# Residual rows and the low halves of the prompt's gates made by accumulating transfers from GpSimd's queue, in a fused two-batch encoder layer

## The chip, the cores and the metric

One NeuronCore of one Trainium2 chip runs the whole program. The metric is the device time of one execution in microseconds (us); lower is better. Times of runs are medians; the profile is of one execution.

Names used throughout: PE is TensorE (matrix multiply), DVE is VectorE, ACT is ScalarE, POOL is GpSimd, SP is SyncE, which issues nearly all the transfers of the kernel. PSUM holds the results of the matmuls, SBUF the operands. A "landing" is the moment when a transfer's data are there and its waiter may go on.

## The reference

Two requests, a prompt of 512 rows and a sample of 1024 rows, go through one encoder layer with shared weights, in float32. After the mixing half of the layer, each request has `x` (rows by 1024). The part that matters here is the gated MLP and what follows it:

```python
h = _rmsnorm(x, norm_ffn_g[l])
u = _dwconv(h @ w_up[l], ffn_dw_w[l], ffn_dw_b[l])              # 1024 -> 5632, conv of 3 taps
x = x + (jax.nn.silu(u[..., :D_FF]) * u[..., D_FF:]) @ w_down[l]  # D_FF = 2816, back to 1024
return _rmsnorm(x, norm_final_g)
```

"Rows of x" are the `x` on the right of the third line: they are added to the down-projection's sums, and the final norm is taken of the result. "The prompt's gates" are `silu(...) * u` of the prompt, the left operand of the down-projection.

## The kernel before, in words

**Exact products from two halves.** PE multiplies a shorter float format (`F32R`). Every float32 operand is therefore split: `hi` is the operand cast to `F32R`, `lo` is operand minus `hi`. A product takes three matmuls: hi by hi, hi by lo, lo by hi. The casts are done by ACT, the subtractions by DVE or POOL.

**The down-projection** is the last phase. It works by a scheme of seven products in place of eight block products: `ORDER = (1, 2, 5, 6, 7, 4, 3)` names them, and product `i` runs over `NPAIR = 11` slices `p` of the contracted dimension. So there are 77 steps `(i, p)`. A step of the first six products has six pieces `tt` of 128 rows: four of the sample and two (`tt` 4 and 5) of the prompt, each of three 128x128 by 128x512 matmuls, 18 matmuls in all (`mm_down`). Product 3 is cut up differently at the end: pieces 0 and 1, with 4 and 5 beside them, slice by slice; then piece 2 over all slices, then piece 3.

**Operands.** `operands(i, p)` makes what a step needs. It splits a block of the sample's gates and a block (or difference of blocks) of `w_down`, both with `split_of`, whose subtraction is DVE's here. At every second `p` it also splits the prompt's gates for two slices at once, 128x512 (128x256 for the last slice): `raw` was loaded by SP from the DRAM tensors `gap...`, ACT casts it to `hi`, POOL writes `lo`. That makes 6 per product, 42 low halves in all, of which 7 are 128x256. The step that is computed is `LEAD` = 4 steps (6 in the later products; `LZ` = 6 slices in product 3) behind the one whose operands are made.

**Slots.** SBUF tiles come from a fixed set of buffers (`Slots`): 61 of 2048 bytes a partition are called `h0` to `h60`, 15 of 4096 bytes `q0` to `q14`, a few others `c` and `d`. A tile takes the longest-free slot of the smallest size that fits, and gives it back when the Python object goes, so a tile's slot is handed on in the order of the program text. In the built program `h7_1997` is the 1997th tile, in slot `h7`. The instruction that writes a slot's next tile waits until the last one's readers are done.

**Rows of x.** The mixing half stored `x` in the DRAM tensors `x1d0` to `x1d11`. Four sums, `o11`, `o12`, `e` and `u`, each three SBUF tiles of 128x1024, collect the products (`evacuate`, after each product's last slice). `load_x1` loads the rows for one sum into three tiles of their own with six transfers of 128x512 from SP; some steps later `with_x` adds them, the first tile by DVE, the others by POOL. The end (`finish`) squares, scales and stores the sums.

**Order.** PE's and SP's instructions stand in the order of the program text in this phase. The orders of ACT, DVE and POOL are set by a scheduler from its own estimates when the program is built. Each engine and each queue carries out its instructions in order: one that waits holds all behind it.

Of the kernel before, what the change touches and what calls it, by code (L numbers as in the profile page):

```python
# [9 lines left out]
F32 = mybir.dt.float32  # L10
F32R = mybir.dt.float32r
BF16 = mybir.dt.bfloat16
AF = mybir.ActivationFunctionType
ALU = mybir.AluOpType
# [4 lines left out]
NT = 512  # L19
# [89 lines left out]
def tile_hybrid_encoder(ctx: ExitStack, tc: tile.TileContext, xs, rel_bias, norm_attn_g, w_in,  # L109
                        attn_sink, conv_dw_w, conv_dw_b, conv_ln_g, conv_ln_b, w_out, norm_ffn_g,  # L110
                        w_up, ffn_dw_w, ffn_dw_b, w_down, norm_final_g, onehot, laid, outs):
    nc = tc.nc
# [8 lines left out]
    sb = Slots(lambda tag: sml if tag[0] == "s" else big,  # L121
               dict(q=(15, 4096), c=(4, 4352), h=(61, 2048), d=(2, 2304), s=(33, 64)))
# [661 lines left out]
    x1d = [dr.tile([P, D], F32, name=f"x1d{i}") for i in range(12)]  # L784
# [56 lines left out]
    def double_keys():  # L841
        for kv in range(NKV):
            for L in range(2):
                nc.gpsimd.tensor_copy(kt[1, kv][L][HD:P, :], kt[1, kv][L][0:HD, :].bitcast(F32))
                yield
# [69 lines left out]
    n, doubling = 0, double_keys()  # L915
# [59 lines left out]
    NPAIR, HT = NJ // 2, NT // 2  # L975
# [94 lines left out]
    def add(out, a, b, eng=None):  # L1070
        (eng or nc.vector).tensor_tensor(out, a, b, op=ALU.add)

    def sub(out, a, b, eng=None):
        (eng or nc.vector).tensor_tensor(out, a, b, op=ALU.subtract)  # L1074

    def split_of(src, dve=False, joint=False):
        if joint and any(f[0][0] == "q" for f in sb.free):
            both = sb.tile([2, NT], F32R, among="q")
            hi, lo = Part(both, 0), Part(both, 1)
        else:  # L1080
            hi, lo = sb.tile([NT], F32R), sb.tile([NT], F32R)
        nc.scalar.copy(hi[:], src)  # L1082
        sub(lo[:], src, hi[:].bitcast(F32), None if dve else nc.gpsimd)
        return hi, lo
# [412 lines left out]
    def load_next(n):  # L1497
        for _ in range(n):
            if ahead:
                key, p = ahead.popleft()  # L1500
                roomy = sum(f[0][0] in "qc" for f in sb.free) > 5
                if (key, p) in second_half:
                    t = second_half.pop((key, p))
                elif key in BRIEF and p % 2 == 0 and p + 1 < NPAIR and roomy:
                    both = sb.tile([2, NT])
                    t, second_half[key, p + 1] = Part(both, 0), Part(both, 1)
                    both = None
                else:
                    t = sb.tile([NT])
                pr[key, p] = t  # L1510
                what, i, n2 = key
                if what == "p":
                    both = next(k for k in gap if i in k)
                    n = min(2, NPAIR - p)
                    nc.sync.dma_start(t[:, 0:n * HT].rearrange("p (n t) -> p n t", t=HT),
                                      gap[both][:, p:p + n, both.index(i), :])
                    continue
                if what == "a":
                    src = ga[i, p][:]
                else:  # L1520
                    src = w_down[0, (2 * p + i) * P:(2 * p + i + 1) * P, n2 * NT:(n2 + 1) * NT]
                nc.sync.dma_start(t[:], src)
# [13 lines left out]
    hl, hp = {}, {}  # L1536

    def operands(i, p):

        while ("a", i, 0) not in [k for k, q in pr if q == p] or (i in need and (need[i], p) not in pr):  # L1540
            load_next(1)
        a = pr.pop((("a", i, 0), p))
        if i == 1:
            b = pr[B11, p]
        elif i == 2:
            b = pr.pop((B21, p))
        elif i == 5:
            b = pr[B12, p]
            sub(b[:], b[:], pr[B11, p][:])
        elif i == 6:  # L1550
            b = pr[B12, p]
            sub(b[:], pr.pop((B22, p))[:], b[:])
        elif i == 7:
            b = pr.pop((B11, p))
            sub(b[:], pr[B12, p][:], b[:])
        elif i == 4:
            b = pr.pop((B21, p))
            sub(b[:], b[:], pr.pop((B12, p))[:])
        else:
            b = pr.pop((B22, p))  # L1560
        joint = i == ORDER[-1]
        hl[i, p] = (split_of(a[:], True, joint), split_of(b[:], True, joint))
        if p % 2 == 0:
            n = min(2, NPAIR - p) * HT
            raw = pr.pop((("p", i, 0), p))
            hi, lo = sb.tile([NT], F32R), sb.tile([NT], F32R)
            nc.scalar.copy(hi[:, :n], raw[:, :n])  # L1567
            sub(lo[:, :n], raw[:, :n], hi[:, :n].bitcast(F32), nc.gpsimd)
            hp[i, p] = hp[i, p + 1] = hi, lo

    steps = [(i, p) for i in ORDER for p in range(NPAIR)]
    LEAD = 4
# [15 lines left out]
    pair2 = lambda: [sb.tile([W2]) for _ in range(3)]  # L1588
    xd = {}

    def load_x1(t, n):
        xd[t, n] = pair2()
        for w in range(3):
            for q in range(2):
                blk = 2 * t + q if w == 2 else 4 + 4 * t + 2 * w + q
                nc.sync.dma_start(xd[t, n][w][:, q * NT:(q + 1) * NT], x1d[blk][:, n * NT:(n + 1) * NT])

    outs_ = {}
    acc = {}
# [21 lines left out]
                add(acc["u"][w][:], z[:], acc["u"][w][:])  # L1621

    def with_x(name, t, n):
        x = xd.pop((t, n))
        for w in range(3):
            add(acc[name][w][:], acc[name][w][:], x[w][:], nc.gpsimd if w else None)

    fins = []

# [41 lines left out]
    def make(k):  # L1671
        nonlocal made
        while made <= min(k, len(steps) - 1):
            i, p = steps[made]
            operands(i, p)
            made += 1
# [5 lines left out]
    def down_step(k):  # L1682
        i, p = steps[k]
        if k > 1:
            next(rest, None)
        load_next(8 if k == 0 else 3 if len(pr) < CAP else 0)
        make(k + (LEAD + max(0, min(2, (k - 60) // 2)) if k else 1))
        late = H2 if i in LATE2 else 0
# [20 lines left out]
        if i == 6 and p == 3:  # L1709
            load_x1(0, 0)  # L1710
        if i == 6 and p == 7:
            with_x("o11", 0, 0)
        if i == 7 and p == XQ[0]:
            load_x1(0, 1)
        if i == 7 and p == XQ[1]:
            with_x("o12", 0, 1)
        if i == 4 and p == XP[0]:
            load_x1(1, 1)
            fins.append(sb.tile([D]))
            nc.sync.dma_start(fins[0][:], norm_final_g.partition_broadcast(P))  # L1720
            nc.scalar.activation(fins[0][:], fins[0][:], AF.Identity, scale=D ** 0.5)
        if i == 4 and p == XP[1]:
            with_x("e", 1, 1)
# [9 lines left out]
    for j in range(2, NJ):  # L1733
# [5 lines left out]
        if j >= NJ - 2:  # L1739
            load_next(4)  # L1740
# [45 lines left out]
    for p in range(NPAIR):  # L1786
# [16 lines left out]
        if p in OTHER:  # L1803
            blk = OTHER[p]
# [83 lines left out]
```

## Time and profile before

| what | value |
|---|---|
| median of 2 runs | 1484.05 us (1483.54 to 1484.55) |
| the profiled execution | 1487.45 us, of which the span of instructions is 1485.0 us |
| mean granted PE clock | 0.997 |
| PE busy | 1467.4 us, 99% of the span |
| DVE, ACT, POOL busy | 1115.4, 807.6, 793.0 us |
| HBM read and written | 166.83 MB and 61.10 MB |

The span runs from the first instruction to the last. Matmuls overlap, so a busy PE is one that always has a matmul under way; how fast they follow each other is their count in a stretch of time. The down-projection takes the stretch from about 1150 us to the end. In rows that group instructions, the columns are line, engine, operation, tiles written and read (slot numbers left out), shapes, count, then busy time and mean duration, then the engine's idle time just before them and what ended it.

### The profile page before, as it was taken

Reading aid. Unit: us, or ns where it says so; the run is one execution under the profiler, and the core shown is the slowest. Engines: PE = TensorE matmul, PEld = TensorE weight load, DVE = VectorE, ACT = ScalarE, POOL = GpSimd, SP = SyncE. Lnnn points to the kernel's source line nnn. Section 1 sums busy time; section 2 is a strip of 40 time slices with the busy share of each in tenths; the row PEclk is TensorE's granted clock in tenths of the full one; section 3 lists DMA queues with packets and bytes.
Section 4 is the critical chain, followed back from the end, with each engine's and each line's share of the span. In section 5 each row is a group of like instructions: output and inputs, shape, how many; then the busy total and the mean of one; then the engine's idle time right before and its main releaser. Section 6 shows DMA issues by size and latency. Waiting matters only on the chain. (4 is left out here: it accounts for less than half of the span.)

```text
span 1485.0 us, 19793 instructions
## 1 busy us (share of the span) xinstructions
PE 1467.4 (99%) x6688; PEld 1207.9 (81%) x6688; DVE 1115.4 (75%) x1500; ACT 807.6 (54%) x1432; POOL 793.0 (53%) x697
## 2 busy tenths in 40 slices
PE   9999999999999999999999999999999999999998
PEld 7788887878888888778887888888888888888886
DVE  6877845649988888675599888888886846578873
ACT  7524555467778776654564545444455553433365
POOL 3564453338779766322546666666655341135556
PEclk9999999999999999999999999999999999999999
DMA  9554331844444454663214433333332395456644
GB/s 369 196 150 144 105 105 31 257 148 142 127 137 136 132 180 142 199 206 127 72 58 142 147 130 129 122 128 122 127 127 94 146 323 168 124 189 220 225 161 162
DMA packets 124625, 228.17 MB, mean 154 GB/s; under 512 B 20420, under 2 KB 45764, under 8 KB 124397
## 3 DMA queue, kind: packets, MB, share of 16 engines
q1 hardware_dynamic: 124092, 226.37, 46.4%
q8 instruction: 52, 0.85, 0.2%
q10 hardware_dynamic: 432, 0.56, 0.1%
q14 instruction: 49, 0.39, 0.1%
HBM read 166.83 MB, written 61.10 MB: 153 GB/s over the span
## 5 line engine op out<-in xcount | busy, mean ns | idle before, releaser
L163 POOL TENSOR_TENSOR q<-q,q 128x1024 fp32r<-128x1024 f32 x66 | 158.7, 2404 | 67.1 <-ACT q L162 43.4
L1074 POOL TENSOR_TENSOR q<-q,q 128x512 fp32r<-128x512 f32 x82 | 125.8, 1542 | 123.0 <-ACT q L1207 112.6
L1074 DVE TENSOR_TENSOR h<-h,h 128x512 fp32r<-128x512 f32 (+1 forms) x161 | 137.7, 887 | 53.3 <-ACT h L1082 21.9
L1586 PE MATMUL w<-h,h 128*128 128x512 f32 x432 | 168.1, 389 | 0.0
L1584 PE MATMUL w<-h,h 128*128 128x512 f32 x432 | 168.1, 389 | 0.0
L1585 PE MATMUL w<-h,h 128*128 128x512 f32 x412 | 160.3, 389 | 0.0
L1074 POOL TENSOR_TENSOR h<-h,h 128x512 fp32r<-128x512 f32 (+1 forms) x46 | 66.7, 1452 | 142.5 <-ACT h L1567 117.8
L1221 PE MATMUL w<-h,q 128*128 128x512 f32 x350 | 138.0, 394 | 1.5 <-ACT w L1292 0.8
L1223 PE MATMUL w<-h,q 128*128 128x512 f32 x350 | 136.4, 390 | 0.2 <-POOL q L1074 0.2
L1222 PE MATMUL w<-h,q 128*128 128x512 f32 x350 | 136.4, 390 | 0.0
L1082 ACT CAST h<-h 128x512 fp32r<-128x512 f32 x116 | 69.1, 619 | 102.2 <-DVE h L1074 27.8
L315 PE MATMUL b<-h,q 128*128 128x512 f32 x312 | 123.0, 395 | 1.3 <-ACT h L461 0.7
L317 PE MATMUL b<-h,q 128*128 128x512 f32 x312 | 122.6, 393 | 0.0
L316 PE MATMUL b<-h,q 128*128 128x512 f32 x312 | 122.3, 392 | 0.0
L315 PE MATMUL u<-h,q 128*128 128x512 f32 x272 | 106.8, 393 | 0.0
L316 PE MATMUL u<-h,q 128*128 128x512 f32 x272 | 106.8, 393 | 0.0
L317 PE MATMUL u<-h,q 128*128 128x512 f32 x272 | 106.7, 392 | 0.0
L352 DVE SCALAR_TENSOR_TENSOR c<-d,cvw,c 128x512 f32<-128x512 f32 x128 | 96.0, 750 | 1.6
L162 ACT CAST q<-q 128x1024 fp32r<-128x1024 f32 x66 | 69.0, 1047 | 51.3 <-PE u L316 15.7
L344 POOL TENSOR_TENSOR h<-h,h 128x512 f32<-128x512 f32 x62 | 82.0, 1324 | 27.8 <-ACT h L343 23.4
L1584 PEld LDWEIGHTS w<-h,h 128*128 128x128 f32 x432 | 81.1, 188 | 16.8
L1586 PEld LDWEIGHTS w<-h,h 128*128 128x128 f32 x432 | 81.1, 188 | 16.7
(464 smaller groups left out, 3990.9 us busy)
## 6 DMA issues: line engine op xcount, KB each, us to landing
q<-in_laid_w_up SPq DMA_DIRECT2D x88, 512.0 KB, 3.7
ga<-q SPq DMA_DIRECT2D x65, 256.0 KB, 2.2
h<-gap SPq DMA_DIRECT2D x57, 256.0 KB, 3.8
h<-ga SPq DMA_DIRECT2D x57, 256.0 KB, 3.5
h<-in_w_down SPq DMA_DIRECT2D x52, 256.0 KB, 3.6
q<-in_laid_w_in SPq DMA_DIRECT2D x22, 512.0 KB, 4.2
gap<-h SPq DMA_DIRECT2D x44, 256.0 KB, 2.4
q<-in_x_sample SPq DMA_DIRECT2D x15, 512.0 KB, 7.0
```

What stands on the lines that cost most here:

```text
L163: (nc.vector if dve else nc.gpsimd).tensor_tensor(lo[:], raw[:], hi[:].bitcast(F32), op=ALU.subtract)
L315: nc.tensor.matmul(out, whi[:, kc, :], hi[:], start=(kc == 0), stop=False)
L316: nc.tensor.matmul(out, whi[:, kc, :], lo[:], start=False, stop=False)
L317: nc.tensor.matmul(out, wlo[:, kc, :], hi[:], start=False, stop=(kc == KC - 1))
L352: nc.vector.scalar_tensor_tensor(acc[:], src(t), w(t), acc[:], op0=ALU.mult, op1=ALU.add)
L1074: (eng or nc.vector).tensor_tensor(out, a, b, op=ALU.subtract)
L1221: nc.tensor.matmul(out, whi[:, s], hi[:], start=(start and c == 0), stop=False, **go)
L1222: nc.tensor.matmul(out, whi[:, s], lo[:], start=False, stop=False, **go)
L1223: nc.tensor.matmul(out, wlo[:, s], hi[:], start=False, stop=(stop and c == 3), **go)
L1584: nc.tensor.matmul(out, sh[:, c], th[:], start=(p == 0 and not seeded), stop=False, **go)
L1585: nc.tensor.matmul(out, sh[:, c], tl[:], start=False, stop=False, **go)
L1586: nc.tensor.matmul(out, sl[:, c], th[:], start=False, stop=(p == NPAIR - 1), **go)
```

## The change

Two edits.

1. The low halves of the prompt's gates. ACT now writes, beside `hi`, a second tile `away` = -`hi`, and GpSimd issues a transfer that reads `away` and adds it to `raw` where it lies. `raw` then holds the low half and is what PE reads. Before, the slot that was given back when `operands` returned was that of `raw`; now it is that of `away`.
2. The rows of x. `load_x1` does nothing. `with_x` issues six accumulating transfers from GpSimd, from `x1d` in DRAM onto the two halves of the three tiles of the sum.

So 42 subtractions on POOL and 12 additions of 128x1024 (4 on DVE, 8 on POOL) go, 24 transfers leave SP's queue, and 42 ACT multiplications and 66 transfers issued by GpSimd come. The program had no transfer issued by GpSimd before.

```diff
@@ load_next
-                    t = sb.tile([NT])
+                    t = sb.tile([NT], F32R if key[0] == "p" else F32)
...
-                    nc.sync.dma_start(t[:, 0:n * HT].rearrange("p (n t) -> p n t", t=HT),
+                    nc.sync.dma_start(t[:, 0:n * HT].bitcast(F32).rearrange("p (n t) -> p n t", t=HT),
@@ operands
-            hi, lo = sb.tile([NT], F32R), sb.tile([NT], F32R)
-            nc.scalar.copy(hi[:, :n], raw[:, :n])
-            sub(lo[:, :n], raw[:, :n], hi[:, :n].bitcast(F32), nc.gpsimd)
-            hp[i, p] = hp[i, p + 1] = hi, lo
+            hi, away = sb.tile([NT], F32R), sb.tile([NT])
+            nc.scalar.copy(hi[:, :n], raw[:, :n].bitcast(F32))
+            nc.scalar.mul(away[:, :n], hi[:, :n].bitcast(F32), -1.0)
+            nc.gpsimd.dma_start(raw[:, :n].bitcast(F32), away[:, :n], accum_op=ALU.add)
+            hp[i, p] = hp[i, p + 1] = hi, raw
@@ load_x1
-        xd[t, n] = pair2()
-        for w in range(3):
-            for q in range(2):
-                blk = 2 * t + q if w == 2 else 4 + 4 * t + 2 * w + q
-                nc.sync.dma_start(xd[t, n][w][:, q * NT:(q + 1) * NT], x1d[blk][:, n * NT:(n + 1) * NT])
+        pass
@@ with_x
-        x = xd.pop((t, n))
         for w in range(3):
-            add(acc[name][w][:], acc[name][w][:], x[w][:], nc.gpsimd if w else None)
+            for q in range(2):
+                blk = 2 * t + q if w == 2 else 4 + 4 * t + 2 * w + q
+                nc.gpsimd.dma_start(acc[name][w][:, q * NT:(q + 1) * NT], x1d[blk][:, n * NT:(n + 1) * NT], accum_op=ALU.add)
```

Two places of the built order show what moves. The names in square brackets are those of the counters that an instruction waits for: an engine's own name, `DMAHW` for transfers issued by SP, `DMASW` for transfers issued by GpSimd.

The first is ACT, in product 6. Before, the low half made from `h41_1921` (`raw`) and `h29_1941` (`hi`) is POOL's, and slot `h41` is next taken by tile `h41_1948`:

```order
L1567 CAST h29_1941_12170<-h41_1921_12116 128x512 [waits DMAHW7_49,DVE_49]
...
L1612 COPY q0_1929_12149<-w0_53_11852 128x1024 [waits PE_49]
L1082 CAST h54_1946_12195<-h47_1943_12188 128x512 [waits DMAHW2_49,DMAHW1_49]
L1567 CAST d0_1957_12230<-h39_1945_12192 128x512 [waits DMAHW4_49]
L1082 CAST h41_1948_12199<-h6_1816_11643 128x512 [waits DVE_49,Pool_49]
```

Now the same place has `h39_1942` as `away`, and slot `h39` is next taken by tile `h39_1948`:

```order
L1567 CAST h5_1941_12190<-h51_1921_12136 128x512 [waits DMASW5_49,DMAHW7_49,DMASW0_49,DVE_49]
...
L1568 ACTIVATE h39_1942_12191<-h5_1941_12190 128x512 [waits Activation_49]
L1609 COPY q0_1929_12149<-w0_53_11868 128x1024 [waits PE_49]
L1082 CAST h37_1946_12216<-h21_1943_12209 128x512 [waits DMAHW2_49,DMAHW1_49]
L1567 CAST d0_1957_12251<-h34_1945_12213 128x512 [waits DMAHW4_49]
L1568 ACTIVATE q1_1958_12252<-d0_1957_12251 128x512 [waits Activation_49]
L1082 CAST h39_1948_12220<-h24_1816_11655 128x512 [waits DMASW2_49,DVE_49]
```

The cast of tile 1948, which belongs to a split of the sample's operands, waited for a POOL subtraction; now it waits for the landing of the transfer that reads `away`, which POOL issues after the multiplication four instructions ahead of it on ACT.

The second is POOL at the start of product 4, where `e` and `u` get their rows of x. Before:

```order
L1071 TENSOR_TENSOR q0_1929_12149<-q3_1755_11388,q0_1929_12149 128x1024 [waits DVE_49]
L1071 TENSOR_TENSOR q14_1928_12148<-q14_1928_12148,c0_2134_13010 128x1024 [waits DMAHW6_49,DMAHW5_49,Pool_49]
L1071 TENSOR_TENSOR q0_1929_12149<-q0_1929_12149,c2_2135_13011 128x1024 [waits DMAHW7_49,DMAHW0_49,Pool_49]
...
L1074 TENSOR_TENSOR h0_2164_13145<-h15_2111_12924,h20_2163_13144 128x512 [waits DMAHW2_49,Activation_49]
L1071 TENSOR_TENSOR q8_1754_11387<-q8_1754_11387,q12_2154_13121 128x1024 [waits DMAHW3_49,DMAHW2_49]
```

Now (of the twelve `L1624` transfers for `e` and `u`, six are shown):

```order
L1624 DMA q13_1927_12167<-x1d9_1281 128x512 [waits DMASW7_49]
L1624 DMA q2_1753_11394<-x1d8_1280 128x512
L1624 DMA q2_1753_11394<-x1d9_1281 128x512 [waits DMASW1_49]
L1071 TENSOR_TENSOR q0_1929_12169<-q3_1755_11396,q0_1929_12169 128x1024 [waits DVE_49]
L1624 DMA q14_1928_12168<-x1d10_1282 128x512 [waits DMASW2_49,Pool_49]
...
L1624 DMA q3_1755_11396<-x1d2_1274 128x512 [waits DMASW0_49]
L1624 DMA q3_1755_11396<-x1d3_1275 128x512 [waits DMASW1_49]
L1569 DMA h34_2104_12943<-h37_2152_13152 128x512 [waits DMASW2_49,DMAHW6_49,PE_49,Activation_49]
```

The additions of x rows stood as single POOL instructions among the low halves; now all twelve transfers for `e` and `u` stand together ahead of the next low half, `L1569`.

## The prediction

> **What bounds the kernel now.** I read the head of the page first, then the table of busy times by stretch for the down-projection, then the waits of PE alone.
>
> ```profile
> span 1485.0 us, 19793 instructions
> PE 1467.4 (99%) x6688; PEld 1207.9 (81%) x6688; DVE 1115.4 (75%) x1500; ACT 807.6 (54%) x1432; POOL 793.0 (53%) x697
> ...
> core 0: us, PE busy (x) PEld busy (x) DVE busy (x) ACT busy (x) POOL busy (x), PEclk, DMA share, GB/s
> 1140.00:1485.00 345.00, 338.52 (x1493) 279.66 (x1491) 234.26 (x260) 153.61 (x280) 144.45 (x118) 1.00 0.57 190
> 1300.00:1460.00 160.00, 160.00 (x708) 132.49 (x707) 122.41 (x123) 71.91 (x145) 83.11 (x63) 1.00 0.59 194
> 1380.00:1420.00 40.00, 40.00 (x178) 33.11 (x177) 34.27 (x30) 12.77 (x24) 25.71 (x12) 1.00 0.79 261
> 1460.00:1485.00 25.00, 18.88 (x84) 15.30 (x82) 9.05 (x10) 9.23 (x21) 13.50 (x19) 0.98 0.46 178
> ...
> PE w L1221 <- ACT w L1292: 0.4, 1, 0.4
> ```
>
> The reader is to see that PE never stands still in the down-projection: 160.00 us of 160, 708 matmuls, one every 160 / 708 = 0.226 us, at the full clock. The last row is the only wait of PE after 1000 us, 0.4 us. So **the ceiling of any gain** is the idle time of PE in the whole span, 1485.0 - 1467.4 = 17.6 us or 1.2%, and in the touched stretch 345.00 - 338.52 = 6.5 us, of which 25.00 - 18.88 = 6.1 us is the drain after the last matmul. The edit touches neither the matmuls nor that drain. What it can do is lose PE's cover.
>
> **What goes.** The rows by shape, of 1180 to 1460 us:
>
> ```profile
> L1074 DVE TENSOR_TENSOR h<-h,h 128x512 fp32r<-128x512 f32 x104 | 91.3, 897 | 34.9 <-ACT h L1082 21.9 <-PE w L1586 5.7 <-POOL h L1074 5.6
> L1074 POOL TENSOR_TENSOR h<-h,h 128x512 fp32r<-128x512 f32 x26 | 36.9, 1421 | 89.7 <-ACT h L1567 75.3 <-DVE h L1074 6.9 <-PE w L1586 6.0
> L1074 POOL TENSOR_TENSOR h<-h,h 128x256 fp32r<-128x256 f32 x7 | 7.1, 1018 | 31.4 <-ACT h L1567 31.4
> L1071 POOL TENSOR_TENSOR q<-q,q 128x1024 f32<-128x1024 f32 x11 | 30.5, 2789 | 14.0 <-DMA q<-x1d 7.6 <-DVE q L1071 4.7 <-DMA h<-gap 1.8
> L1071 DVE TENSOR_TENSOR q<-q,q 128x1024 f32<-128x1024 f32 x4 | 6.8, 1706 | 3.7 <-DMA q<-x1d 3.7
> L1082 ACT CAST h<-h 128x512 fp32r<-128x512 f32 x106 | 63.0, 619 | 101.0 <-DVE h L1074 27.8 <-PE w L1585 21.4 <-DMA h<-ga 18.3
> L1662 ACT ACTIVATE q<-q,s 128x512 f32<-128x512 f32 x6 | 4.3, 719 | 1.1 <-POOL s L1656 1.1
> L1074 DVE TENSOR_TENSOR q<-q,q 128x512 f32<-128x512 f32 x2 | 1.4, 692 | 0.1
> ```
>
> - POOL loses 35 x 1.42 + 7 x 1.02 = 57 us of low halves and 8 x 2.79 = 22 us of x additions.
> - DVE loses 4 additions, 6.8 us, and their 3.7 us of waiting for x.
> - DVE's own subtractions take 0.897 us where 0.692 us is to be had (last row); if POOL's reading is what stretches them, up to 104 x 0.2 = 21 us of DVE time comes back over 280 us.
> - SP loses 24 issues.
>
> None of it is on PE's path, so all of it together is worth 0 us; it only lowers the price of what comes.
>
> **What comes, and is hidden.** ACT gets 42 multiplications; the nearest row is the scaling ACTIVATE, 0.719 us: at most 42 x 0.72 = 30 us, beside 345.00 - 153.61 = 191 us of idle ACT. The x transfers onto `o11` and `o12` are waited for only by the end, tens of us later; those onto `u` by the DVE additions that close product 4, nine steps and more away, at least 9 x 18 x 0.226 = 36 us. POOL's total falls if an issue costs under 79 / 66 = 1.2 us.
>
> **What comes, and isn't hidden: a slot.** `away` gives its slot back at once, and the free list is so short that the next tile in it is often only a few instructions away. In the built order, of the 42 multiplications, 16 have on ACT the next tile of their slot within five instructions (the place in product 6 shown above is one: four), and 13 with those where DVE's next instruction has it stand in the stretch from 1300 us to the end of product 3's loading. That instruction waited for a POOL subtraction before; the profile has these waits already:
>
> ```profile
> ACT h L1082 <- POOL h L1074: 15.2, 7, 5.1
> DVE h L1074 <- POOL h L1074: 5.6, 3, 2.4
> ```
>
> Ten waits, 20.8 us, and PE didn't notice. Now it waits for an issue on POOL and a landing. The trace has no transfer issued by GpSimd and none that accumulates, so both are bounded from the rows of SP's transfers (the last number is the median from issue to landing) and of the x loads:
>
> ```profile
> q1 hardware_dynamic: 33936, 54.28, 58.7%
> h<-gap SPq DMA_DIRECT2D x36, 256.0 KB, 4.2
> q<-x1d SPq DMA_DIRECT2D x18, 256.0 KB, 5.1
> out_sample<-q SPq DMA_DIRECT2D x3, 256.0 KB, 2.0
> ...
> L1596 SPq DMA_DIRECT2D q<-x1d x18: 319/430/460, 1309.7 to 1406.3; - x18
> DMA to landing us min/median/max: 3.3/5.4/7.1
> ```
>
> *Landing:* from 2.0 us (a store) to 7.1 us (the longest x load); if the old contents were read in a second pass, to twice 5.1 = 10.2 us. I take 5.0 us, near the x loads, because the added traffic falls on queues that are already 0.59 busy on average and 0.79 in the dense stretch: 35 x 0.262 + 7 x 0.131 = 10 MB more on 54.3 MB is 11 points, and twice that if the target is read too. *Issue on POOL:* from 0.43 us (SP's) to 1.42 us (the subtraction it replaces); I take 1.0 us, between them.
>
> [...]
>
> **The sum.** Casts behind an exposed multiplication cover about three ACT instructions, 3 x 0.62 = 1.9 us. So an exposed place stands 1.0 + 5.0 - 1.9 = 4.1 us. Thirteen of them in the stretch: 53 us. DVE, which feeds and is fed by ACT, has 160 - 122.4 = 37.6 us of idle time there to catch up in; I count half, 19 us, since the other half lies where nothing is late (none counted, the loss grows by 19; all counted, it is gone). PE is fed four steps ahead: 4 x 18 x 0.226 = 16 us of cover, which is used up once. 53 - 19 - 16 = **18 us**. Against the profiled execution, 1487.45, that is 1505; its time is 3.4 us over the median of the runs, 1484.05, so the forecast for the median is 1484 + 18 = **1502 us**. Under 2% (30 us, about what a measurement of this kernel can tell from no change).
>
> **The rivals.**
>
> 1. *Hidden after all.* If issue and landing are 0.43 + 2.3 us (about a store's), a place stands 0.8 us, 13 places 11 us, less than DVE's idle time: 1484, between 1481 and 1487. For it: ten such waits hide now. Against it: every row of a load into SBUF is 3.5 us or more in this stretch.
> 2. *Slower: the landing is long.* One mechanism, the same slots. At 1.4 + 7.1 us a place stands 6.6 us; 13 x 6.6 - 35 = 51 us, 1535. At 1.4 + 10.2 us it is 9.7 us and 91 us, 1575. It passes 2% from 30 + 35 = 65 us over 13 places, 5.0 us each, so from issue plus landing of 6.9 us. For it: the 0.79 in the dense stretch, and that an accumulation has two things to read. Against it: source and target of the 42 are both in SBUF, and stores land in 2.0 us.
> 3. *Slower: POOL's queue becomes the bound* at the start of product 4. Twelve issues and three additions stand ahead of the next low half, in place of three and two additions: 12 x issue + 8.4 - 14.0 us. With the 16 us of cover it decides from an issue of (16 + 5.6) / 12 = 1.8 us; at 3 us it is 14 us there and 13 x 2 = 26 us at the slots, on top of 18: 1542. Against it: 0.43 us on SP.
> 4. *A gain.* DVE's returned time pulls nothing forward, since PE has no idle time but the ceiling above: 1478 to 1484 at best.
>
> [...]
>
> **How the numbers follow.** Chances: the forecast's mechanism between 1488 and 1513, 0.33; rival 1, 0.24; rival 2, 0.32; rival 3, 0.08; rival 4, 0.03. The likeliest case's own range is 1488 to 1513. The range from 1482 to 1568 leaves out the upper end of rival 2 (about 0.07) and a gain. Within 2% are the forecast, rivals 1 and 4 and a little of 3: 0.59; slower 0.40; faster by over 2% is beyond the ceiling: 0.01.
>
> **What would show it.** In the profile after: waits of ACT's `L1082` and DVE's `L1074` for DMA `h<-h` (or `d`, `c`) of some 4 us each, about sixteen; PE with idle time for the first time between 1300 and 1460 us, waiting for DVE or ACT; DVE's subtractions nearer 0.7 than 0.9 us; issue to landing of the `L1569` transfers near 5 us. It is wrong if PE stays at 160 of 160 (rival 1), if PE's first waits are for a DMA or behind `L1624` (rival 3), or if the places that wait are not the slots but the low halves themselves: the last one is made at 1452 us,
>
> ```profile
> 1452.02 0.74 POOL L1074 TENSOR_TENSOR h<-h,h 128x256 fp32r<-128x256 f32 x1
> ```
>
> and is first read about 72 matmuls before PE's end at 1460 + 18.88 = 1478.9, so near 1462.6: 10 us of cover against 0.7 + 1.0 + 5.0 - 0.7 = 6 us more.

## The result, and the profile after

The changed kernel takes 1503.49 us (1500.88 and 1506.11) against 1484.05: a ratio of 1.0134, 95% interval 1.009 to 1.0178. It is slower by 19 us, under 2%, as forecast (1502). The profiled execution took 1500.88 us. One of e4's eleven runs below was in the slow state (2466.87 us at a granted clock of 0.556) and is left out of its ratio.

Head of the page, PE's waits after 1000 us, and busy times by stretch (columns as before):

```profile
span 1499.1 us, 19923 instructions
PE 1471.0 (98%) x6688; PEld 1210.9 (81%) x6688; DVE 1077.7 (72%) x1496; ACT 829.0 (55%) x1474; POOL 773.6 (52%) x713
...
PE w L1585 <- DVE q L1071: 9.7, 3, 6.7
PE w L1587 <- DMA h<-h: 2.6, 1, 2.6
...
1300.00:1460.00 160.00, 148.84 (x633) 121.80 (x632) 85.39 (x109) 68.07 (x125) 51.71 (x50) 0.96 0.78 201
1140.00:1485.00 345.00, 332.67 (x1442) 273.77 (x1441) 189.36 (x249) 169.64 (x311) 108.84 (x127) 0.98 0.75 210
```

PE, which never stood between 1300 and 1460 us, now works 148.84 of those 160 us. After 1000 us it stands three times for DVE's `L1071`, the addition that empties a finished product's PSUM banks (the evacuation), and once for a low half itself. DVE and POOL are less busy than before, as intended (POOL 108.84 us in the stretch, from 144.45). The span grew by 14.1 us: PE's idle time by 10.5 (1499.1 - 1471.0 = 28.1, from 17.6) and its busy time by 3.6 for the same 6688 matmuls. Those 3.6 us go with the granted clock, 0.994 on the mean where it was 0.997.

Here is how one stall is built, by the timelines of ACT, DVE and PE (start, duration; in brackets the wait ahead of it and what ended it), and the clock behind it:

```profile
1376.13 0.63 ACT L1568 ACTIVATE h<-h 128x512 f32<-128x512 f32 x1 [2.51 <-DMA h<-h]
...
1383.18 0.62 ACT L1082 CAST h<-h 128x512 fp32r<-128x512 f32 x1 [4.52 <-DMA h<-h]
1383.83 0.69 DVE L1074 TENSOR_TENSOR h<-h,h 128x512 fp32r<-128x512 f32 x1 [3.85 <-ACT h L1082]
...
1395.26 1.22 DVE L1071 TENSOR_TENSOR q<-w,q 128x1024 f32<-128x1024 f32 x1
...
1396.54 0.79 PE L1585 MATMUL w<-h,h 128*128 128x512 f32 x1 [6.67 <-DVE q L1071]
1397.13 0.63 PE L1586 MATMUL w<-h,h 128*128 128x512 f32 x1
1397.55 0.63 PE L1587 MATMUL w<-h,h 128*128 128x512 f32 x1
...
1396.40:1400.10 3.70, 3.56 (x8) 2.81 (x9) 3.70 (x6) 1.06 (x1) 3.54 (x2) 0.50 0.67 153
```

A multiplication and a cast stand 2.51 and 4.52 us for the landing of an `away` in their slots, the subtractions behind them start late, and the evacuation stands behind those in DVE's order; PE waits for the evacuation. Then the clock is at 0.50 and matmuls start 0.42 us apart (1397.13 to 1397.55) in place of 0.226.

Three of the waits for a landing, by ACT's timeline, and then their sums by the waits from 1180 us on (total, times, longest):

```profile
1330.42 1.14 ACT L1082 CAST h<-h 128x512 fp32r<-128x512 f32 x2 [2.67 <-DMA h<-h]
1349.60 1.66 ACT L1082 CAST h<-h 128x512 fp32r<-128x512 f32 x3 [2.82 <-DMA h<-h]
1432.84 0.62 ACT L1082 CAST h<-h 128x512 fp32r<-128x512 f32 x1 [11.92 <-DMA h<-h]
...
ACT h L1082 <- DMA h<-h: 26.5, 6, 11.9
DVE h L1074 <- DMA h<-h: 3.9, 3, 1.9
ACT h L1568 <- DMA h<-h: 3.8, 2, 2.5
```

They are where the forecast put them, but 11 in place of 16, most under 4 us, and one of 11.92. That one isn't like the others. Its transfer was issued right behind the 12 x transfers of product 4 (POOL's timeline, and the landing times in us of `L1569` and `L1624`, least, median, most):

```profile
1402.15 3.59 POOL L1624 DMA_DIRECT2D q<-x1d  x4
...
1406.76 8.60 POOL L1624 DMA_DIRECT2D q<-x1d  x8
1416.85 0.86 POOL L1569 DMA_DIRECT2D h<-h  x1 [1.50 <-DMA h<-in_w_down]
...
DMA to landing us min/median/max: 2.6/4.6/16.0
...
DMA to landing us min/median/max: 4.3/9.2/16.3
...
1432.86 0.50 PE L1587 MATMUL w<-h,h 128*128 128x512 f32 x1 [2.61 <-DMA h<-h]
```

1416.85 + 16.0 is 1432.8: there the cast starts that wanted the slot, and, by the last row, at the same moment PE, which stood for the low half itself. POOL's issuing wasn't what held this low half: POOL had stood idle for 1.50 us ahead of it, for a load. The transfers' own cost shows in the queues' rows (packets, MB, share of 16 engines), from 1180 to 1470 us:

```profile
q1 hardware_dynamic: 30048, 47.20, 48.3%
q0 software_dynamic: 8640, 14.95, 29.9%
```

POOL's accumulating transfers take 29.9 / 14.95 = 2.0 points of the engines' time for each MB, SP's copies 48.3 / 47.20 = 1.0.

### The profile page after: what moved, and what is told of

Same layout as the page of the kernel before. It is cut to its first block, busy times and chain, and to the rows that moved or that the text cites. A ratio compares the mean times of both kernels' runs of the same rounds, so it can differ in the third digit from the quotient of the medians.

```text
span 1499.1 us, 19923 instructions
## 1 busy us (share of the span) xinstructions
PE 1471.0 (98%) x6688; PEld 1210.9 (81%) x6688; DVE 1077.7 (72%) x1496; ACT 829.0 (55%) x1474; POOL 773.6 (52%) x713
## 5 line engine op out<-in xcount | busy, mean ns | idle before, releaser
L1074 DVE TENSOR_TENSOR h<-h,h 128x512 fp32r<-128x512 f32 (+1 forms) x161 | 115.8, 752 | 110.2 <-ACT h L1082 65.2
L1585 PE MATMUL w<-h,h 128*128 128x512 f32 x424 | 167.1, 394 | 7.8 <-DVE q L1071 7.8
L1587 PE MATMUL w<-h,h 128*128 128x512 f32 x438 | 172.1, 393 | 2.6 <-DMA h<-h 2.6
L1586 PE MATMUL w<-h,h 128*128 128x512 f32 x414 | 162.8, 393 | 0.0
L1569 POOL DMA_DIRECT2D h<-h x37 | 34.0, 918 | 177.0 <-ACT h L1568 116.1
L1082 ACT CAST h<-h 128x512 fp32r<-128x512 f32 x116 | 69.5, 618 | 93.0 <-DMA h<-h 26.5
```

What stands on the lines that cost most here:

```text
L1585: nc.tensor.matmul(out, sh[:, c], th[:], start=(p == 0 and not seeded), stop=False, **go)
L1586: nc.tensor.matmul(out, sh[:, c], tl[:], start=False, stop=False, **go)
L1587: nc.tensor.matmul(out, sl[:, c], th[:], start=False, stop=(p == NPAIR - 1), **go)
```

## The experiments

Three theories: **A, the slot** (ACT or DVE stands for a landing, because `away` hands its slot on at once); **B, the load** (accumulating takes double engine time, so everything lands later); **C, POOL's queue** (low halves stand behind the x issues). Each experiment was timed in five rounds beside the kernel before (4 to 11 runs); the row of the change has its two runs. The us in the table are the ratio less one, times 1483. The plain and the half transfers leave out additions; their kernels are there for the time alone.

| kernel | low halves | x | slots of `away` | median us | ratio, 95% interval | us |
|---|---|---|---|---|---|---|
| the change | accumulating | accumulating | handed on | 1503.49 | 1.0134 (1.009 to 1.0178) | +20 |
| e1 | accumulating | as before | handed on | 1502.92 | 1.0122 (1.0104 to 1.0139) | +18 |
| e2 | as before | accumulating | none | 1493.27 | 1.0064 (1.0052 to 1.0077) | +9 |
| e4 | plain | plain | handed on | 1485.5 | 1.0013 (1.0004 to 1.0022) | +2 |
| e9 | accumulating | plain | handed on | 1490.31 | 1.0049 (1.0036 to 1.0062) | +7 |
| e10 | plain | accumulating | handed on | 1492.76 | 1.0062 (1.005 to 1.0074) | +9 |
| e6 | accumulating, half the columns | accumulating | handed on | 1501.08 | 1.0122 (1.0104 to 1.014) | +18 |
| e3 | accumulating | accumulating | three own | 1509.16 | 1.0165 (1.0149 to 1.0182) | +24 |
| e7 | plain | plain | three own | 1499.04 | 1.01 (1.0086 to 1.0114) | +15 |
| e8 | accumulating | accumulating | given back later | 1505.98 | 1.0155 (1.0141 to 1.0168) | +23 |
| e12 | accumulating | accumulating | three own, to product 4 | 1495.44 | 1.0074 (1.0059 to 1.0088) | +11 |
| e11 | as before, and a load | as before | none | 1495.02 | 1.0078 (1.0065 to 1.009) | +12 |
| e5 | as before, and a load | as before | none | 1553.89 | 1.0473 (1.0458 to 1.0487) | +70 |

### Each part alone: e1 and e2

```diff
 e1: with_x and load_x1 as before the change; CAP = 23
 e2: operands() and load_next() as before the change
```

> Only the low halves are made by accumulating transfers; the rows of x are loaded and added as before (the planner's cap on loaded tiles is 23 instead of 24, so that the slots suffice). Theory A (the slot of `away` is handed on at once, and ACT or DVE stands for the landing): this part holds nearly the whole loss, 12 to 20 us over the kernel before, 1496 to 1504. Theory B (the accumulating transfers take twice the time of the DMA engines, and the weight loads land late): the low halves add 10.1 MB at 2.0 points, 20 of the 26 points that the whole change adds, so three quarters of 19 us: about 15 us, 1499. Theory C (the x transfers stand ahead of low halves in POOL's queue): at most 5 us, under 1489.

> Only the rows of x are added by accumulating transfers; the low halves are POOL's subtractions as before. Theory A: no slot of `away`, so within 3 us of the kernel before, 1481 to 1487. Theory B: 6.3 MB go from 1.0 to 2.0 points each, 6 of the 26 points, so about 5 us, 1489. Theory C: most of the loss is here, 10 to 19 us, 1494 to 1503.

Both parts cost, and neither A nor C alone gives both. Without any `away`, e2 loses 9 us; PE's main stall in it, by the chain of waits, begins with two loads of SP's:

```profile
1429.44 4.35 DMA h<-in_w_down
1433.87 0.63 ACT h L1082
...
1435.85 2.61 DMA h<-ga
1439.07 1.14 ACT h L1082 x2
...
1442.12 1.23 DVE q L1071
1443.40 0.80 PE w L1584
```

Weights and gates that land late feed the same chain: cast, subtraction, evacuation, PE. e1 loses nearly as much as the whole change, though it has no x transfers of POOL's. It is no clean half: its x tiles hold slots, and POOL's additions return, beside five of which in a row a single subtraction on DVE lasted 11.57 us. And some of its loss is its own: by PE's waits it stands 3.5 us at 1182 us for DVE's `L1339`, and 1.0 us for ACT's `L1607`, which no other run does.

```profile
PE w L1585 <- DVE q L1339: 3.5, 1, 3.5
```

### Accumulating or plain, in the same order: e4, e9 and e10

The orders, the slots and the number of issues are those of the change; the plain transfers overwrite.

```diff
-nc.gpsimd.dma_start(raw[...], away[...], accum_op=ALU.add)    # e4, e10
+nc.gpsimd.dma_start(raw[...], away[...])
-nc.gpsimd.dma_start(acc[name][w][...], x1d[blk][...], accum_op=ALU.add)    # e4, e9
+nc.gpsimd.dma_start(acc[name][w][...], x1d[blk][...])
```

> The whole change, its 66 transfers as plain copies that overwrite their target (the additions are left out). The order, the slots and POOL's issues stay. Theory A: the slot is still waited for, for issue plus a landing of perhaps 3 us instead of 4.6, so the loss shrinks by a third at most: 1494 to 1500. Theory B: the added engine time falls from 26 points to 10, so the loss falls to about 7 us, 1491, and the weight loads land as early as before (near 3.5 us, not 4.4). Theory C: unchanged, 1498 to 1506, since the issues stay.

> The whole change in its own order and slots, the 42 low halves by accumulating transfers, the 24 x transfers as plain copies that overwrite (the additions of x are left out). Slot theory (A): the places near 1330, 1349, 1383 us stand as with the change; what changes is the one near 1432 us, whose low half was issued right behind the burst of 12 accumulating x transfers: its wait falls from 11.9 to about 5 us if the burst delayed it. Then about half the loss goes: 1491 to 1497. Theory of the load (B): 6 of the 16 extra points go, so 1494 to 1499. If the x transfers have no part in it: 1499 to 1506.

> The whole change in its own order and slots, the 24 x transfers accumulating, the 42 low halves as plain copies that overwrite (the subtraction is left out). If the burst of x transfers makes the loss, by the queue or by the engines: the wait near 1432 us stays at 8 us or more and the time at 1492 to 1500. If the low halves' own landing makes it (A): 1485 to 1489.

With plain copies PE loses nothing: 280 us of 280 from 1180 to 1460. So 66 plain issues on POOL (0.55 us each), the slots and the moved order together cost some 2 us (0.6 to 3.3 by the interval); **accumulating costs**. The queue's rows of e4 (1180 to 1470 us), and ACT's waits in the two places in e4, e9 and e10:

```profile
q0 software_dynamic: 4656, 15.08, 13.7%
...
1374.90 0.62 ACT L1082 CAST h<-h 128x512 fp32r<-128x512 f32 x1 [3.17 <-DMA h<-h]
1419.07 0.62 ACT L1082 CAST h<-h 128x512 fp32r<-128x512 f32 x1 [2.80 <-DMA h<-h]
```

```profile
1379.25 0.62 ACT L1082 CAST h<-h 128x512 fp32r<-128x512 f32 x1 [5.47 <-DMA h<-h]
1417.78 0.62 ACT L1082 CAST h<-h 128x512 fp32r<-128x512 f32 x1 [0.40 <-DMA h<-h]
```

```profile
1379.45 0.62 ACT L1082 CAST h<-h 128x512 fp32r<-128x512 f32 x1 [3.14 <-DMA h<-h]
1427.77 0.62 ACT L1082 CAST h<-h 128x512 fp32r<-128x512 f32 x1 [12.61 <-DMA h<-h]
```

The first place follows the low halves' own kind (5.47 accumulating, 3.1 plain), the second follows the x transfers' kind (12.61 with accumulating x, though the low half is a plain copy there; 0.40 and 2.80 with plain x). Singly the two parts cost 7 and 9 us, together 20; the surplus of some 4 us over their sum lies within the interval of the change's own two runs.

The wait in the first place doesn't set the size of the stall behind it alone. In e9 the cast stands longer than in the change, 5.47 us against 4.52, but PE then stands 2.24 us, not 6.67:

```profile
1393.23 0.80 PE L1585 MATMUL w<-h,h 128*128 128x512 f32 x1 [2.24 <-DVE q L1071]
```

The change has the other wait of 2.51 us just ahead of it, and it came there late: its two casts `L1567` ahead of both waits start at 1372.40 us, those of e9 at 1370.13. Nor does B's other sign hold, that weights land early again in e4: SP's loads of `in_w_down` land there after a median of 4.6 us, against 4.4 with the change, and yet e4 loses only 2 us.

What delays the second place, queue or engines? The DMA issues of the 19 us behind the start of the 12 x transfers, and the busy times there: in the change from 1403 us, then in e4, where they start 8 us earlier, from 1395 us (KB each, median us to landing):

```profile
q<-x1d POOLq DMA_DIRECT2D x12, 256.0 KB, 11.6
h<-ga SPq DMA_DIRECT2D x6, 256.0 KB, 12.6
h<-in_w_down SPq DMA_DIRECT2D x6, 256.0 KB, 16.1
...
h<-h POOLq DMA_DIRECT2D x2, 256.0 KB, 15.0
...
1403.00:1422.00 19.00, 19.00 (x86) 15.73 (x85) 13.30 (x13) 8.17 (x16) 14.50 (x16) 1.00 0.99 223
```

```profile
q<-x1d POOLq DMA_DIRECT2D x12, 256.0 KB, 5.5
h<-ga SPq DMA_DIRECT2D x7, 256.0 KB, 7.0
h<-in_w_down SPq DMA_DIRECT2D x7, 256.0 KB, 8.5
...
1395.00:1414.00 19.00, 19.00 (x85) 15.73 (x84) 12.98 (x16) 9.46 (x18) 10.17 (x17) 1.00 0.95 345
```

SP's loads, on another queue, land as late as POOL's, 12.6 and 16.1 us after issue, where they take 7.0 and 8.5 beside plain copies. So it isn't POOL's queue alone: the engines are all but full in both, but a share of 0.99 moves 223 GB/s in the change and one of 0.95 moves 345 in e4. Theory C falls, B holds for this place; whether the order within POOL's queue adds to it isn't separated.

### Size and load: e6, e11 and e5

```diff
 e6:
-nc.gpsimd.dma_start(raw[:, :n].bitcast(F32), away[:, :n], accum_op=ALU.add)
+nc.gpsimd.dma_start(raw[:, :n // 2].bitcast(F32), away[:, :n // 2], accum_op=ALU.add)
 e11, in the kernel before, behind POOL's subtraction of a low half:
+nc.gpsimd.dma_start(spare[...][:, :n], hi[:, :n].bitcast(F32), accum_op=ALU.add)
 e5, at the same place:
+nc.gpsimd.dma_start(spare[...][:, :2 * n], w_down[0, 0:P, 0:2 * n])
```

> The whole change, but each of the 42 transfers for the low halves covers only the left half of its columns (the right half of the low halves keeps the raw rows). Order, slots and number of issues stay; x as in the change. Theory A: the slot is waited for nearly as long, 1496 to 1502. Theory B: the engine time of the low halves falls from about 20 points to 10; the x part keeps its 10 us, and the 19 us of the gates fall by more than half: 1492 to 1497.

> The kernel before, with 42 accumulating transfers that nobody waits for: each time POOL has subtracted a low half, it issues an accumulating transfer of the high half onto a spare place in DRAM. The order of the work, POOL's subtractions and the x loads stay. Load on the DMA engines alone (B): 8 to 15 us, 1492 to 1499, the weight loads landing later by a half to one us. Slot alone (A): 1483 to 1488.

> The kernel before, with a load added that nobody waits for: behind each of the 42 low halves, which POOL still subtracts, POOL issues a plain copy of 512 KB (256 KB for the last of a product) from the weights to a spare place in DRAM. By the rows of the accumulating transfers (30.2% of the engines for 15 MB, against 13.7% as plain copies) that is about the engine time of the 42 accumulating ones. No slot, no accumulation, order and waits as before. Theory A (the slot): no loss beyond the issues, 1483 to 1487. Theory B (the load on the DMA engines): 12 to 20 us, 1495 to 1503, with PE waiting behind DVE as in the run with the gates alone.

Halving the low halves' bytes saves nothing that shows (e6). B as I had put it, by bytes over the whole stretch, missed this: the halved transfers still land after a median of 4.3 us where whole ones took 5.0 in that stretch, and the place behind the burst still stands 10.1 us. In e11 a load that nobody waits for, 42 accumulating transfers, costs 12 us with no `away` at all, and SP's weight loads land after 5.2 us (3.5 before); it also puts 42 issues of 0.87 us on POOL beside its subtractions, and the two aren't separated. e5 says nothing on the stretch: its copies depend on nothing and were issued between 1.7 and 83.6 us, and PE worked 66.43 us of the first 130 there (127.81 before).

### The slots: e3, e7, e8 and e12

```diff
 e3, e7 (plain transfers) and, up to product 4, e12:
-hi, away = sb.tile([NT], F32R), sb.tile([NT])
+if len(own) < 3:
+    own.append(sb.tile([NT]))
+else:
+    own.rotate(-1)
+hi, away = sb.tile([NT], F32R), own[-1]
 e8: the last three tiles away are held in a queue before they are given back
```

> The whole change, but `away` has three slots of its own, used in turn, that are handed to no other tile; the next multiplication in the same slot comes some 24 us later. The traffic and POOL's queue stay; all other tiles have three slots fewer. Theory A: the casts and subtractions no longer stand for a landing, and the time falls to 1484 to 1490. Theory B: the same load on the DMA engines, so 1498 to 1506 as with the change. Theory C: also 1498 to 1506.

> The three own slots of `away` together with plain copies that overwrite (the additions are left out): what the three slots fewer cost without the engine time of accumulating. If the load makes the loss of 26 us with the own slots, it falls to 1484 to 1488 here. If the own slots bring a loss of their own (the last stretch waits, and the waits show POOL's order there), it stays at 1492 or more, and the rest, up to 16 us, is the load's.

> The whole change, but `away` gives its slot back three low halves later, so that nobody stands for a landing just issued; of the 42, those with ACT's next tile of the slot within five instructions fall from 13 to 4. Traffic and POOL's issues stay. Theory A: 1485 to 1492. Theory B: 1498 to 1506. Both in equal parts: 1492 to 1498.

> The whole change, all 66 transfers accumulating, but `away` has three slots of its own, used in turn, up to product 4; for the last product, 3, it takes and gives back a slot as in the change. With the slots back by then, the last stretch should not get the 11 us wait that the own slots brought before. The waits for a landing near 1330, 1349 and 1383 us are gone by construction; the transfers of product 3 still stand behind the burst of x transfers. Theory A: the stall of 6.8 us near 1390 us goes, and what is left is the place behind the burst, 2 to 5 us and the low clock after it: 1489 to 1495. Theory B (the load alone, by the run with the transfers to DRAM): the slots were no part of it, and the time stays at 1499 to 1506.

e3 looked like the end of theory A. It wasn't a fair test: with three slots fewer the last stretch gets a stall of its own, as PE's waits in e3 and in e7 show.

```profile
PE w L1590 <- ACT w L1646: 13.3, 2, 10.9
```

```profile
PE w L1590 <- ACT w L1646: 11.0, 1, 11.0
```

In e7 that 11.0 us is PE's only wait of the down-projection, so the own slots cost it, not the load; between e7 and e3, with the same order, lie the 10 us that accumulating costs without a slot handed on. e8 has the same last-stretch wait (11.0 us) and tells no more. e12 gives the slots back in time and has no such wait. Its PE waits and its longest ACT wait:

```profile
PE w L1595 <- DVE q L1071: 3.8, 2, 2.2
PE w L1597 <- DMA h<-h: 3.4, 1, 3.4
...
1430.68 0.62 ACT L1082 CAST h<-h 128x512 fp32r<-128x512 f32 x1 [9.86 <-DMA h<-h]
```

The waits near 1330, 1349 and 1383 us are gone, the stall behind them is 2.2 us where it was 6.7, and the time is 8 us lower; the place behind the burst stays, since there PE waits for the low half and not for the slot. The intervals (up to 1.0088 here, from 1.009 for the change) just part, so the size is uncertain: about 8 of the 19 us are put down to slots handed on, and the rest comes with slots of their own as well. Not all of the 8 need be the slots: the order was built anew for e12, and e9, with the slots handed on, has a stall of 2.2 us at this place too.

## Why the prediction was right, and where its steps weren't

**Right in part of the mechanism.** A cast or subtraction that stands for a landing in the slot of `away`, and PE that then waits for DVE, is what was forecast, and the stretch is nearly so (a first stall, of 1.17 us, falls before it, at 1252 us). The evacuation as the link between them wasn't in the text, and by e12 the slots account for about 8 of the 19 us. The moved work cost next to nothing: e4 has all of it, ACT's 42 multiplications among it (0.63 us each), and loses 2 us. DVE's subtractions came down to 0.737 us from 0.897. The ceiling of the gain held: with accumulating taken away, nothing is won.

**Issue and landing** were sized well at the median: an issue takes 0.87 us (1.0 forecast), a landing 4.6 (5.0). The longest landing, 16.0 us, lies beyond the 10.2 that the text took as the far end. The plain copies of e4 landed after a median of 4.2 us in this traffic.

**The sum came out right by luck: its errors cancel.** Failed step one: 13 places at 4.1 us, 53 us. ACT and DVE stood 26.5 + 3.9 + 3.8 = 34 us in 11 places, one of them with 11.92. Failed step two: the two deductions. By them, 34 - 19 - 16 would be no loss at all; yet in the profiled execution PE stood 10.5 us longer and 3.6 us went with the clock. In the stall near 1396 us DVE's idle time didn't catch up, with 13 subtractions between the late cast and the evacuation, and the cover of 16 us by `LEAD`, which makes operands ahead, doesn't take in the evacuation, which can't be done ahead.

**Failed step three: "the x transfers are hidden".** Nobody waits for them, but they fill the DMA engines (a share of 0.99 in the 19 us behind the start of the 12): e2 and e10 lose 9 us by them. The text had this price ("twice that if the target is read too"; it is twice) and used it only to place the landing time, not to ask what else lands late while 12 such transfers run. Rival 3 named the right moment, the start of product 4, but for a reason (an issue of 1.8 us) that isn't the one: an issue took 0.87 us, and POOL stood idle before the low half behind the burst.

**Not forecast:** the low clock (0.50) behind three of the four stalls, and that PE would stand for a low half itself (2.6 us) behind the burst; the text had watched the last low half alone.

What stays open: how much of the rest is late weights and how much the low half's own landing, since the same full engines make both; whether the order within POOL's queue adds to it, how much of e12's 8 us is its own order, and why e1 loses 18 us and e9 only 7 (4.5 us of e1's are the two waits that it has alone).

## What to carry to other kernels

A transfer that accumulates took the DMA engines twice the time of a copy of the same bytes here (2.0 points for each MB, 0.91 as plain copies): count that against the share in the stretch where it runs, and ask what else must land there, above all when it is issued in a burst that no dependency spreads. A tile that feeds a transfer shouldn't hand its slot to the next instruction of an engine that others wait for; but slots of its own must come out of somewhere, so look at the last stretch before believing either. When PE waits for an evacuation, read what stands ahead of it in DVE's order too.

## What was not expected of the hardware

- **Accumulating.** 2.0 points of engine time for each MB against 0.91 as plain copies by the same queue (13.7 / 15.08, e4), with 8640 packets for 14.95 MB against 4656 for 15.08; the issue takes 0.87 us against 0.55 on POOL.
- **The clock.** In the profile of the change it is at 0.50 in stretches of 3.70, 3.30 and 3.20 us behind the stalls of 6.67, 2.61 and 1.89 us, and stays at 1.00 behind the one of 1.17. Half of their mean of 3.4 us, about 1.7 us, is lost by such a stretch, nearly as much again as by a stall of 2 us. The length of the stall alone doesn't decide: behind 1.89 us the change's clock is at 0.50, behind 2.24 us e12's is at 1.00, and in e9, behind a stall as long as e12's, the first matmul takes 0.80 us, as behind the change's longest (0.79, at 0.50). Part of the spread between runs goes with the clock: e12's lie between 1492.4 us at a mean of 0.998 and 1497.45 at 0.993. The rows are of the stretch behind the change's last stall, and behind e12's of 2.24 us:

```profile
1451.18 0.63 PE L1585 MATMUL w<-q,h 128*128 128x512 f32 x1 [1.89 <-DVE q L1071]
...
1451.50:1454.70 3.20, 3.20 (x9) 2.43 (x9) 2.89 (x4) 2.35 (x5) 0.86 (x1) 0.50 0.02 5
```

```profile
1394.00:1397.40 3.40, 3.40 (x15) 2.80 (x16) 3.40 (x3) 1.53 (x2) 3.40 (x2) 1.00 0.77 213
```
